# The fifth score matmul of an attention: a low-part key of 64 rows, filled up to 128 rows with zeros

## The chip, the core and the metric

The kernel runs on one core of a Trainium2 chip. The metric is the time of one execution on the device in microseconds (us), lower is better. Engines are named as in the profile: PE is TensorE's matmul stream, PEld its loads of the stationary operand, DVE is VectorE, ACT is ScalarE, POOL is GpSimd, SP is SyncE, whose queue issues most of the transfers.

## What is computed

A trunk of two layers on 512 tokens of width 2048, in float32. A layer normalises the stream, projects it, feeds three groups of heads (a gated spatial mixing A, a gated short convolution B, a latent attention C), projects the result back and adds a gated embedding. The change sits in the attention C, with 8 heads and a rotary key that all heads share:

```python
def latent_attention(q, c_kv, k_rope, z, cos, sin, kv_gain, w_ukv, qn_g, qr_g, kn_g, kr_g):
    q_nope = rms_norm(q[..., :C_NOPE], qn_g)                                # 128 features
    q_rope = apply_rope(rms_norm(q[..., C_NOPE:], qr_g), cos, sin)          # 64 features
    k_nope, v = ...                                                         # 128 features each, per head
    k_r = apply_rope(rms_norm(k_rope, kr_g), cos, sin)                      # 64 features, one for all heads
    ...
    s = jnp.einsum('bqhd,bkhd->bhqk', qn, k_nope) + jnp.einsum('bqhr,bkr->bhqk', qr, k_r)
    w = jax.nn.softmax(s.astype(jnp.float32) * scale, axis=-1)
    return jnp.einsum('bhqk,bkhd->bqhd', w, v)
```

## The kernel before

To keep float32's precision, every operand of a matmul is split into two parts of the type float32r, a high part (the rounded value, written by ACT) and a low part (what the rounding left, written by DVE). A product is then three matmuls into one PSUM bank: high by high, high by low, low by high (`mm3`, L164 to L167). Most weights are 128 x 512 tiles that come by SP's queue into five buffers (`raw`), and are split into six buffers each of `whi` and `wlo` (L144, L145).

The scores of one head for 128 queries against all 512 keys are one bank (`scores`, L606): three matmuls for the 128 features without rotation (L612 to L614) and two for the 64 rotary features (L615, L616). For these two the queries lie in `q2`, whose rows 0 to 63 are the high part and whose rows 64 to 127 are the low part of the same 64 features, and the key in `krh`, which holds the high part twice, one copy under the other. So L615, over 128 rows, makes high by high and low by high at once. L616 makes the remaining product, the high query by the low key `krl`, over rows 0 to 63 alone. In both the piece of `q2` is the stationary operand and the key is the moving one. There are 2 layers, 8 heads and 4 blocks of queries, so 64 of these banks, and L615 and L616 run 64 times each.

`krh` and `krl` are made once a layer, in `queries(0)`, long before the attention. `krl` is a tile of 128 x 512, of which only the upper 64 rows are written.

Around the scores, a generator `fillers` supplies units of 12 matmuls that don't depend on the attention (the gate z_c, and A's and B's share of the output projection); they are placed between the steps of a head by hand (`ST`, `FN`). A scheduler then sets the order of instructions on each engine, so score matmuls and fillers alternate in places. Each engine runs its own instructions in that order and waits on semaphores for the others. POOL's part in the queries is the power -1/2 of the norms (`rpow`, L232), and it issues the transfers of the attention.

Of the kernel before, what the change touches and what calls it, by code (L numbers as in the profile page):

```python
# [33 lines left out]

# columns of the input projection
OFF_U, OFF_V, OFF_ZA = 0, 512, 1024
# [8 lines left out]

# columns of the packed per-partition parameters of a layer
C_ATTN, C_PLE, C_OUT, C_KVN, C_QN, C_KN, C_CW, C_CB, C_BS = 0, 16, 32, 48, 52, 53, 54, 66, 70
NCOL = 74
# columns of the packed free-dimension gains of a layer
R_SGU, R_QR, R_KR = 0, 512, 576  # L50
NROW = 640

# 1 / 10000 ** (arange(0, 64, 2) / 64) in float32
INV_FREQ = [
# [9 lines left out]

# whole turns taken off units of 2**16 and 2**2 radians
TURNS = {2.0 ** 16: 0.37835047045272496, 2.0 ** 2: 0.6366197723675814}

NU, RAWB, HIB, SB = 62, 5, 6, 3
# units of filling work: at the start of the attention, and at the steps of a head
ST, FN = (4, 4, 4, 4, 4), (2, 1, 1, 1, 1)  # L70
# tiles of A and B that come back after each quarter of the last filler that reads the normalised input
FETCH = ((0, 1, 2, 3), (4, 5, 6, 7), (), ())
# [13 lines left out]
def trunk(ctx, tc, xT, pT, pos, freq, pars, rows, wsp, wckv, wv, w512, wq0, wq, wkv, wout, wgate, wple, outT):  # L86
# [52 lines left out]

# [1 line left out]
    def split(src, gain=None, hi=None, lo=None):  # L141
        """src (SBUF or PSUM, f32), times a per-partition gain, as two f32r parts."""
        if gain is None:
            a.copy(hi, src)  # L144
            v.tensor_tensor(out=lo, in0=src, in1=hi.bitcast(F32), op=ALU.subtract)  # L145
        else:
            a.activation(out=hi, in_=src, func=AF.Copy, scale=gain)
            v.scalar_tensor_tensor(out=lo, in0=src, scalar=gain, in1=hi.bitcast(F32),  # L148
                                   op0=ALU.mult, op1=ALU.subtract)
# [19 lines left out]
    def groupT(srcs, xs, evac, tags=("mm",)):  # L169
        """out^T: for each 128 features a bank [features, 512 tokens]; a weight unit is 4 k tiles of them."""  # L170
        nq = len(xs) // 4
        for f in range(len(srcs)):
            ps = bank(tags[f % len(tags)])
            for q in range(nq):
                wh, wl = weight(srcs[f][q], S)
                for i in range(4):
                    c = slice(i * P, (i + 1) * P)
                    k = 4 * q + i
                    mm3(ps, wh[:, c], wl[:, c], xs[k][0], xs[k][1], k == 0, k == len(xs) - 1)
            evac(f, ps)  # L180

    def groupK(srcs, load, evac):
        """the same for 4 banks at a time, a k tile at a time; a weight unit is a k tile of 512 features."""
        pb = [bank(t) for t in NB]
        for i, src in enumerate(srcs):
            xh, xl = load(i)
            wh, wl = weight(src, S)
            for f in range(4):
                c = slice(f * P, (f + 1) * P)
                mm3(pb[f], wh[:, c], wl[:, c], xh, xl, i == 0, i == len(srcs) - 1)  # L190
        for f in range(4):
            evac(f, pb[f])

    def groupN(srcs, xs, n, evac):
        """out: 4 banks [128 tokens, n features]."""
        pb = [bank(t) for t in NB]
        for i, (src, (xh, xl)) in enumerate(zip(srcs, xs)):
            wh, wl = weight(src, n)
            for t in range(NT):
                c = slice(t * P, (t + 1) * P)  # L200
                mm3(pb[t][:, :n], xh[:, c], xl[:, c], wh[:, :n], wl[:, :n], i == 0, i == len(xs) - 1)
        for t in range(NT):
            evac(t, pb[t][:, :n])

    class Stat:
        """sum over features (partitions and tiles) of squares, for each token."""

# [13 lines left out]
        def mean(self, n, eps=EPS):  # L221
            """[128 tokens, 4] of mean + eps"""
            ps = bank()
            for t in range(NT):
                pe.matmul(ps[:, t:t + 1], self.acc[:, t * P:(t + 1) * P], ones[:, 0:1], start=True, stop=True)
            m = small(NT, "mean")
            v.tensor_scalar(out=m, in0=ps[:, 0:NT], scalar1=1.0 / n, scalar2=eps, op0=ALU.mult, op1=ALU.add)
            return m
# [6 lines left out]
    def tokrow(r):  # L235
        """[128 tokens, 4] -> the same numbers along the free dimension of every partition."""
        rd = drp.tile([S], F32, name=nm("rd"))
        g.dma_start(rd.rearrange("(t p) -> p t", p=P), r)
        rt = lay.tile([P, S], F32, tag="rT", name=nm("rT"), bufs=2)
        g.dma_start(rt, rd.partition_broadcast(P))  # L240
        return rt

# [1 line left out]
    def tables():  # L244
# [41 lines left out]
        v.tensor_tensor(out=turn, in0=turn, in1=r, op=ALU.subtract)  # L286
        # radians of the coarse pieces and of the rest, then whole turns off
        v.scalar_tensor_tensor(out=turn, in0=turn, scalar=2.0 * math.pi, in1=ang, op0=ALU.mult, op1=ALU.add)
# [17 lines left out]
    def rope_gains(row, cos, sin, scale, s):  # L306
        """cos and sin times the gains of the halves that they meet."""
        out = []
# [9 lines left out]
    def rope(x, tabs, nh, outs):  # L318
        """x [P, NT, nh, 64]; outs: for each head a tile [P, NT, 2, 64], the result twice."""
        c1, s2, c2, s1 = tabs  # L320
# [15 lines left out]
    def transpose4(src):  # L336
        """four [128, 128] blocks -> one bank, side by side."""
        ps = bank()
        for t in range(NT):
            pe.transpose(ps[:, t * P:(t + 1) * P], src(t), ident)  # L340
        return ps

# [1 line left out]
    st = Stat()  # L344
# [12 lines left out]
    for L in range(DEPTH):  # L357
# [3 lines left out]

# [1 line left out]
        ck = []  # L363
# [8 lines left out]
        rT = tokrow(rN)  # L372
        # the sums lack rN: mean of the normalised input's squares is rN^2 times theirs
        m = st_k.mean(RANK, 0.0)
# [14 lines left out]

# [1 line left out]
        vh = [U("vh", F32R) for _ in range(4)]  # L391
        vl = [U("vl", F32R) for _ in range(4)]

        def rms_parts(ps, scale, segs):
            """1 / rms of the segments (offset, count, width) of scale * ps, times scale"""
            n = sum(s[1] for s in segs)
# [51 lines left out]
        def normed(tiles, r, k0):  # L448
            """normalised, with their gain, in two parts, out of the way until the output projection"""
            rt = tokrow(r)  # L450
            for i, y in enumerate(tiles):
                v.tensor_tensor(out=y, in0=y, in1=rt, op=ALU.mult)
                hi, lo = T("yh", "n", F32R), T("yl", "n", F32R)
                split(y, C(C_OUT + k0 + i), hi, lo)
                sync.dma_start(ydram[k0 + i, 0], hi.bitcast(F32))
                sync.dma_start(ydram[k0 + i, 1], lo.bitcast(F32))
# [6 lines left out]

# [1 line left out]
        if L == 0:  # L465
# [8 lines left out]
        def queries(p):  # L474
# [22 lines left out]
            if nk:  # L497
# [3 lines left out]
                a.copy(krh, ps)  # L501
                v.tensor_tensor(out=krl[0:ROPE], in0=ps[0:ROPE], in1=krh[0:ROPE].bitcast(F32), op=ALU.subtract)

# [1 line left out]
        yb = [U("yb") for _ in range(4)]  # L505
# [38 lines left out]

# [1 line left out]
        def ev_zc(f, ps):  # L546
# [6 lines left out]
        def kv(h):  # L553
            """in two parts"""
            kn = U("kn")
# [50 lines left out]
        def scores(h, half):  # L606
            (kh, kl), _, _, (qh, ql), q2 = side[h]
            pn = []
            for t in (2 * half, 2 * half + 1):
# [5 lines left out]
                pe.matmul(ps, q2[:, o], krh, start=False, stop=False)  # L615
                pe.matmul(ps, q2[0:ROPE, o], krl[0:ROPE], start=False, stop=True)  # L616
                mx = small(1, "mx")
# [12 lines left out]
        def weightsT(pn):  # L630
            """half of the queries' weights transposed, two key tiles to a bank"""
            out = []
# [34 lines left out]

        # z_c, and the share of A and B in the output projection, by units that fill the gaps of the attention
        def fillers():
# [78 lines left out]

# [1 line left out]
        st_p = Stat()  # L750
# [8 lines left out]

        # the share of C lacks its norm, which comes when it is added  # L760
        def ev_out(k, ps):
# [16 lines left out]

# [1 line left out]
        rT = tokrow(rpow(st_p.mean(D), NT))  # L780
# [32 lines left out]
def _ftiles(w):  # L813
    """[K, F] -> [F / 128, K / 512, 128, 4 * 128]: for 128 features, 4 k tiles side by side"""
    k, n = w.shape
# [58 lines left out]
```

## Time and profile before

| | |
|---|---|
| time, median of 3 runs | 2226.69 us (2224.87 to 2227.31) |
| profiled execution: span | 2231.2 us |
| PE busy | 2206.7 us (99%), 10720 matmuls |
| PEld busy | 1868.3 us (84%) |
| DVE, ACT, POOL busy | 1121.1 (50%), 906.4 (41%), 218.4 us (10%) |
| mean granted TensorE clock | 0.998 |

The profiled execution is known by its span alone, from its first to its last instruction; it is one execution, and it is 4.5 us longer than the median of the runs. Busy time of PE is not time at its peak: matmuls overlap in the pipeline, so one that takes 390 ns can start 227 ns after the one before. What the stream of matmuls costs is therefore read from the distances of their starts. The attention's scores run from about 560 to 820 us in the first layer and from about 1668 to 1932 us in the second.

### The profile page before, as it was taken

The numbers are of one execution on the slowest core, as the hardware profiler recorded it, in microseconds if no ns is written. First come the engines' busy times: TensorE is split into PE (matmuls) and PEld (weight loads), VectorE is DVE, ScalarE is ACT, GpSimd is POOL, SyncE is SP. The second block draws the span as 40 slices with busy tenths as digits, with TensorE's granted clock in tenths as the row PEclk, the third lists the DMA queues.
The fourth block names the chain that finished last, engine by engine and source line by source line (L and its number), as shares of the span: only waits on it lengthen the run. The fifth ranks groups of instructions, "written<-read, shape, count | busy, mean of one in ns | idle before, by whom it ended". The sixth has DMA issues, their size and how long they took to land.

```text
span 2231.2 us, 29725 instructions
## 1 busy us (share of the span) xinstructions
PE 2206.7 (99%) x10720; PEld 1868.3 (84%) x10720; DVE 1121.1 (50%) x2326; ACT 906.4 (41%) x1709; POOL 218.4 (10%) x331
## 2 busy tenths in 40 slices
PE   8999999999999999999999999999999999999999
PEld 6888888988888878888888888889888888888887
DVE  7444354435556655665533434444354566566433
ACT  6332333324565553443332323233246655434222
POOL 0000000002121101100000000000021221011000
PEclk9999999999999999999999999999999999999999
DMA  6333534435354444444333345334453544344432
GB/s 211 100 105 92 136 99 116 117 67 190 103 174 138 124 128 111 130 152 118 118 97 106 95 81 161 90 107 118 97 170 99 176 133 133 109 129 129 137 115 71
DMA packets 142739, 272.22 MB, mean 122 GB/s; under 512 B 17328, under 2 KB 34112, under 8 KB 142592
## 3 DMA queue, kind: packets, MB, share of 16 engines
q1 hardware_dynamic: 122256, 214.83, 33.8%
q0 software_dynamic: 18032, 51.30, 7.7%
q10 hardware_dynamic: 2304, 4.20, 0.6%
q8 instruction: 84, 1.38, 0.3%
q14 instruction: 63, 0.52, 0.1%
HBM read 234.58 MB, written 35.67 MB: 121 GB/s over the span
## 4 chain that ended last, share of the span: by engine, by line
PE 73%; DMA 3%; issue 1%; DVE 1%; ACT 0%; POOL 0%; DVEq 0%; ACTq 0%; POOLq 0%
PE mm L165 13%; PE mm L166 13%; PE mm L167 13%; PE s L167 6%; PE s L165 6%; PE s L166 6%; PE o L167 2%; PE o L166 2%; PE o L165 2%; PE tr L638 1%; PE s L616 1%; DMA ydram<-yh 1%; PE tr L340 1%; DMA rd<-rs 1%; PE s L612 1%
## 5 line engine op out<-in xcount | busy, mean ns | idle before, releaser
L145 DVE TENSOR_TENSOR wlo<-raw,whi 128x512 fp32r<-128x512 f32 (+2 forms) x754 | 501.9, 669 | 625.5 <-ACT whi L144 608.1
L144 ACT CAST whi<-raw 128x512 fp32r<-128x512 f32 (+2 forms) x754 | 449.0, 603 | 854.1 <-PE mm L166 433.0
L165 PE MATMUL mm<-hi,whi 128*128 128x512 f32 x1312 | 513.2, 391 | 3.3 <-DVE pt L387 3.3
L166 PE MATMUL mm<-lo,whi 128*128 128x512 f32 x1312 | 511.3, 390 | 0.0
L167 PE MATMUL mm<-hi,wlo 128*128 128x512 f32 x1312 | 511.1, 390 | 0.0
L165 PEld LDWEIGHTS mm<-hi,whi 128*128 128x128 f32 x1312 | 246.4, 188 | 55.1 <-issue 3.5
L167 PEld LDWEIGHTS mm<-hi,wlo 128*128 128x128 f32 x1312 | 246.3, 188 | 51.6
L166 PEld LDWEIGHTS mm<-lo,whi 128*128 128x128 f32 x1312 | 246.4, 188 | 49.5
L165 PE MATMUL s<-hi,whi 128*128 128x512 f32 x480 | 184.5, 391 | 6.8 <-ACT whi L144 5.7
L166 PE MATMUL s<-lo,whi 128*128 128x512 f32 x480 | 187.6, 391 | 1.0 <-DVE lo L148 1.0
L167 PE MATMUL s<-hi,wlo 128*128 128x512 f32 x480 | 186.4, 390 | 0.0
L166 PE MATMUL s<-wlo,hi 128*128 128x384 f32 (+2 forms) x480 | 170.6, 355 | 8.5 <-DVE wlo L145 8.5
L165 PE MATMUL s<-whi,hi 128*128 128x384 f32 (+2 forms) x480 | 169.7, 354 | 0.0
L167 PE MATMUL s<-whi,lo 128*128 128x384 f32 (+2 forms) x480 | 169.5, 353 | 0.0
L232 POOL TENSOR_TENSOR rs<-ms,mhalf 128x1 f32<-128x1 f32 (+2 forms) x104 | 87.6, 848 | 743.4 <-DVE ms L405 717.0
L165 PEld LDWEIGHTS s<-hi,whi 128*128 128x128 f32 x480 | 90.4, 189 | 25.7 <-ACT whi L144 5.7
L166 PEld LDWEIGHTS s<-lo,whi 128*128 128x128 f32 x480 | 90.6, 189 | 20.4 <-DVE lo L148 1.4
L167 PEld LDWEIGHTS s<-hi,wlo 128*128 128x128 f32 x480 | 90.1, 188 | 18.6
L166 PEld LDWEIGHTS s<-wlo,hi 128*128 128x128 f32 x480 | 90.9, 189 | 16.1 <-DVE wlo L145 10.7
L165 PE MATMUL mm<-yh,whi 128*128 128x512 f32 x256 | 103.1, 403 | 0.0
L167 PE MATMUL mm<-yh,wlo 128*128 128x512 f32 x256 | 100.4, 392 | 0.0
L166 PE MATMUL mm<-yl,whi 128*128 128x512 f32 x256 | 100.4, 392 | 0.0
(231 smaller groups left out, 3203.6 us busy)
## 6 DMA issues: line engine op xcount, KB each, us to landing
raw<-in_w_dram SPq DMA_DIRECT2D x256, 256.0 KB, 2.7
raw<-in_wout_dram SPq DMA_DIRECT2D x128, 256.0 KB, 2.8
raw<-in_wgate_dram SPq DMA_DIRECT2D x128, 256.0 KB, 2.7
raw<-in_wq_dram SPq DMA_DIRECT2D x96, 192.0 KB, 2.4
raw<-in_wckv_dram SPq DMA_DIRECT2D x32, 256.0 KB, 2.8
raw<-in_wv_dram SPq DMA_DIRECT2D x32, 256.0 KB, 2.7
raw<-in_wkv_dram SPq DMA_DIRECT2D x32, 256.0 KB, 2.8
mdram<-old SPq DMA_DIRECT2D x32, 256.0 KB, 2.0
```

What stands on the lines that cost most here:

```text
L144: a.copy(hi, src)
L145: v.tensor_tensor(out=lo, in0=src, in1=hi.bitcast(F32), op=ALU.subtract)
L165: pe.matmul(out, lh, rh, start=start, stop=False)
L166: pe.matmul(out, lh, rl, start=False, stop=False)
L167: pe.matmul(out, ll, rh, start=False, stop=stop)
L232: g.tensor_tensor(out=r, in0=m, in1=mhalf[:, 0:n], op=ALU.pow)
L340: pe.transpose(ps[:, t * P:(t + 1) * P], src(t), ident)
L612: pe.matmul(ps, qh[:, o], kh, start=True, stop=False)
L616: pe.matmul(ps, q2[0:ROPE, o], krl[0:ROPE], start=False, stop=True)
L638: pe.transpose(ps[:, j * HS + i * P:j * HS + (i + 1) * P], pn[i][:, c], ident)
```

## The change

`queries(0)` gets one more instruction: POOL writes zeros into rows 64 to 127 of `krl`. The fifth score matmul takes all 128 rows of `q2` and of `krl`: the low part of the query meets the zeros, so the sum is the same as before. Comments and docstrings go as well, which moves the lines from L504 on by one (L616 becomes L617).

```diff
                 a.copy(krh, ps)
                 v.tensor_tensor(out=krl[0:ROPE], in0=ps[0:ROPE], in1=krh[0:ROPE].bitcast(F32), op=ALU.subtract)
-
-        # ---- B: gated short convolution ----
+                g.memset(krl[ROPE:P].bitcast(F32), 0.0)
+
+
         yb = [U("yb") for _ in range(4)]
...
                 pe.matmul(ps, q2[:, o], krh, start=False, stop=False)
-                pe.matmul(ps, q2[0:ROPE, o], krl[0:ROPE], start=False, stop=True)
+                pe.matmul(ps, q2[:, o], krl, start=False, stop=True)
                 mx = small(1, "mx")
```

On PE, at the first bank of scores that is completed, the order before is this (`s` is the bank of scores, `mm` that of a filler; a row is line, operation, out<-inputs and the elements written):

```order
L166 MATMUL mm_5006<-lo_510,whi_5063 128x512
L167 MATMUL mm_5006<-hi_509,wlo_5064 128x512
L615 MATMUL s_5083<-krh_1763,q_4879 128x512
L616 MATMUL s_5083<-krl_1764,q_4879 128x512
L612 MATMUL s_5097<-hi_4799,hi_4870 128x512
L613 MATMUL s_5097<-lo_4800,hi_4870 128x512
```

In the changed kernel the same place reads as follows.

```order
L166 MATMUL mm_5007<-lo_510,whi_5064 128x512
L167 MATMUL mm_5007<-hi_509,wlo_5065 128x512
L616 MATMUL s_5084<-krh_1763,q_4880 128x512
L617 MATMUL s_5084<-krl_1764,q_4880 128x512 [waits Pool_49]
L613 MATMUL s_5098<-hi_4800,hi_4871 128x512
L614 MATMUL s_5098<-lo_4801,hi_4871 128x512
```

Nothing has moved on PE in the whole program; the first fifth matmul of a layer has a semaphore of POOL to wait for, and line numbers and tile numbers have gone up by one. On POOL, in the second layer, the place between the norms of `queries(0)` (`128x5`) and those of `queries(1)` (`128x4`) was before:

```order
L232 TENSOR_TENSOR rs_12502<-ms_12497,mhalf 128x5 [waits DVE_49]
L232 TENSOR_TENSOR rs_12517<-ms_12512,mhalf 128x5 [waits DVE_49]
L232 TENSOR_TENSOR rs_13164<-ms_13159,mhalf 128x4 [waits DVE_49,Activation_49]
L232 TENSOR_TENSOR rs_13178<-ms_13173,mhalf 128x4 [waits DVE_49,Activation_49]
L232 TENSOR_TENSOR rs_13192<-ms_13187,mhalf 128x4 [waits DVE_49]
```

And in the changed kernel:

```order
L232 TENSOR_TENSOR rs_12503<-ms_12498,mhalf 128x5 [waits DVE_49]
L232 TENSOR_TENSOR rs_12518<-ms_12513,mhalf 128x5 [waits DVE_49]
L503 MEMSET krl_11837 64x512 [waits PE_49,Pool_49]
L232 TENSOR_TENSOR rs_13166<-ms_13161,mhalf 128x4 [waits DVE_49,Activation_49,Pool_49]
L232 TENSOR_TENSOR rs_13180<-ms_13175,mhalf 128x4 [waits DVE_49,Activation_49]
```

The memset stands between the two groups, and in the second layer it waits for PE (the last reader of the buffer's contents of before). The first layer has it in the same place, without the wait for PE. No other row of DVE, ACT, POOL or SP has another place than before.

## Rows read from the trace of the kernel before

**Rows 1.** Head of the page, and its part 1: busy time of the engines.

```profile
span 2231.2 us, 29725 instructions
## 1 busy us (share of the span) xinstructions
PE 2206.7 (99%) x10720; PEld 1868.3 (84%) x10720; DVE 1121.1 (50%) x2326; ACT 906.4 (41%) x1709; POOL 218.4 (10%) x331
```

**Rows 2.** Busy time by stretches; (x) instructions, PEclk granted clock, DMA share, GB/s.

```profile
560.00:945.00 385.00, 385.00 (x1983) 317.65 (x1982) 228.25 (x488) 202.54 (x395) 59.71 (x100) 1.00 0.44 130
1667.00:1945.00 278.00, 278.00 (x1501) 228.80 (x1501) 161.49 (x376) 159.74 (x323) 48.34 (x80) 1.00 0.43 133
```

**Rows 3.** Tile krl: its instructions, duration ns min/median/max, idle time before.

```profile
L616 PEld LDWEIGHTS s<-krl,q x64: 182/183/183, 572.6 to 1932.4; 64*128 64x128 f32 x64
L616 PE MATMUL s<-krl,q x64: 491/498/502, 572.6 to 1932.4; 64*128 64x512 f32 x64
L502 DVE TENSOR_TENSOR krl<-tr,krh x2: 681/682/683, 294.1 to 1399.7; 64x512 fp32r<-64x512 f32 x2
...
  issue: 20.8, 64
```

**Rows 4.** Line L615: duration ns min/median/max.

```profile
L615 PEld LDWEIGHTS s<-krh,q x64: 186/188/190, 572.1 to 1931.8; 128*128 128x128 f32 x64
L615 PE MATMUL s<-krh,q x64: 388/397/502, 572.3 to 1932.0; 128*128 128x512 f32 x64
```

**Rows 5.** Timeline of PE around the first fifth matmul: start us, us, line.

```profile
565.29 0.39 PE L167 MATMUL mm<-hi,wlo 128*128 128x512 f32 x1
...
572.09 0.39 PE L167 MATMUL mm<-hi,wlo 128*128 128x512 f32 x1
572.31 0.39 PE L615 MATMUL s<-krh,q 128*128 128x512 f32 x1
572.63 0.50 PE L616 MATMUL s<-krl,q 64*128 64x512 f32 x1
573.06 0.50 PE L612 MATMUL s<-hi,hi 128*128 128x512 f32 x1
573.39 0.39 PE L613 MATMUL s<-lo,hi 128*128 128x512 f32 x1
```

**Rows 6.** Timeline of PEld, same place; in brackets idle before it.

```profile
572.63 0.18 PEld L616 LDWEIGHTS s<-krl,q 64*128 64x128 f32 x1 [0.35 <-issue]
573.06 0.19 PEld L612 LDWEIGHTS s<-hi,hi 128*128 128x128 f32 x1 [0.25 <-issue]
```

**Rows 7.** Timeline of PE, another place, three fifth matmuls close together.

```profile
680.61 0.47 PE L615 MATMUL s<-krh,q 128*128 128x512 f32 x1
...
683.50 0.40 PE L166 MATMUL mm<-yl,whi 128*128 128x512 f32 x1
```

**Rows 8.** Waits of PEld, 560 to 945 us: total us, times, longest.

```profile
PEld s L616 <- issue: 10.4, 32, 0.4
PEld mm L165 <- issue: 3.4, 14, 0.2
...
```

**Rows 9.** Waits of all engines, 560 to 945 us.

```profile
ACT whi L144 <- PE mm L166: 54.0, 36, 3.0
```

**Rows 10.** Timeline of all engines, 652 to 662 us; in brackets idle before it.

```profile
652.92 0.72 ACT L147 ACTIVATE hi<-yc,par 128x512 fp32r<-128x512 f32 x1 [1.60 <-DVE yc L654]
...
661.00 0.36 ACT L573 ACTIVATE kn<-mm,rs 128x128 f32<-128x128 f32 x1
...
662.01 0.27 PE L340 MATMUL tr<-ident,kn 128*128 128x128 f32 x1
```

**Rows 11.** Groups of POOL's instructions by form: busy us, mean ns.

```profile
L125 POOL MEMSET ones<- 128x128 f32 x1 | 0.2, 202 | 0.0
L127 POOL MEMSET mhalf<- 128x32 f32 x1 | 0.1, 121 | 0.0
```

**Rows 12.** Timeline of POOL, second layer, between queries(0) and queries(1).

```profile
1461.55 1.98 POOL L232 TENSOR_TENSOR rs<-ms,mhalf 128x4 f32<-128x4 f32 x2 [72.96 <-DVE ms L405]
```

## The prediction

> **What bounds the kernel now.** I read the page's head first: a span of 2231.2 us with PE busy for 2206.7 us of it, so PE sits without a matmul for 24.5 us in all, while no other engine is busy for more than half [rows 1]. Then the table by stretches, for the two in which the scores run: PE is busy for 385.00 of 385.00 us and for 278.00 of 278.00 us, at a granted clock of 1.00, which is the upper level, 2.4 GHz [rows 2]. There nothing is late for PE; what counts is how fast its matmuls follow one another. Busy time doesn't show that, since matmuls overlap, so the third view is the list by line, and the fourth the timeline, from which I take distances of starts.
>
> The list by line sets L616 and L615 side by side. Both write 128 x 512 outputs with 512 moving columns and the same `q2` block as stationary operand. L616 reads half the rows, yet takes 491 to 502 ns where L615 has a median of 397 ns; its weight load is the same as the other's, 183 against 188 ns, but stands behind 20.8 us of idle time of the loads in 64 cases, 0.325 us each, with nothing waited for that the profile shows ("issue") [rows 3, 4].
>
> **What a fifth matmul costs now.** An undisturbed matmul of 512 columns first: from the L167 at 565.29 to that at 572.09 us there are 30 matmuls, so 6.80 / 30 = 0.227 us from start to start [rows 5]. Then around the first L616: L615 starts at 572.31, L616 at 572.63 (0.32 later), L612 at 573.06 (0.43), L613 at 573.39 (0.33). These three steps last 1.08 us; three undisturbed ones would last 3 x 0.227 = 0.68. So 0.40 us is lost around one L616 [rows 5].
>
> The loads say how. In a run of 128-row matmuls a load lies beside the matmul before it. The load for L616 comes at 572.63, together with its own matmul and 0.32 us after L615's start, and the load for L612 at 573.06, again together with its matmul; both have idle time ahead (0.35 and 0.25 us) [rows 6]. So when the stream goes from 128 rows to 64 and when it goes back, PE no longer loads ahead, as if the running matmul had to come to its end first; the load is exposed, twice per L616. That it is the number of rows I take from what else differs: L615 and L616 have the same stationary block, engine and bank, and no semaphore is named ahead of L616. That a bank is finished by it isn't it either: the L167 at 572.09 ends a filler's bank, and L615 follows 0.22 us later [rows 5].
>
> The Trainium skill, "TensorEngine Tiling (Array Packing)", section "Key Properties", says that a change of the tiling mode drains TensorE, and "Available Configurations" has 64 x 128 among the modes; the trace agrees, 0.40 us around one pair of changes. The same notes say in "TensorE: Matmul & The Clock Gate", section "LDWEIGHTS (loading the stationary operand)", that a load's time goes by its columns and not by the contraction, which speaks against the change; the trace agrees for the load itself (183 and 188 ns), so by this rule alone the time would stay 2226.7 us.
>
> It is so in all 64 places. In the first layer's stretch the loads of L616 have 10.4 us of "issue" in 32 cases, and behind them stands, beside the score matmuls that follow, L165 of a filler with 3.4 us in 14 [rows 8]. Where three L616 stand close together, with an L615 between each two, the time from the first L615 (680.61) to the L166 behind the third (683.50) is 2.89 us for seven steps, against 7 x 0.227 = 1.59. Of the 1.30 us between them about 0.10 belongs to the transposes ahead, after which the first L615 takes 0.47 us in place of 0.39; the other 1.2 us are three times 0.40 [rows 7].
>
> **The change part by part.** (1) The fifth matmul takes 128 rows, as its neighbours do. It then has the shape, the operands' types and the place of L615, and I cost it as an undisturbed matmul: 0.227 us, and no pause on either side. That is 64 x 0.40 = 25.6 us off PE's stream. The order on PE is the same, so nothing else is gained or lost there. Its bounds: read to 0.01 us the three steps may be 1.07 or 1.09, so 64 x 0.39 = 25.0 and 64 x 0.41 = 26.2 us. (2) The zeros: one memset a layer on POOL. POOL's memsets show 202 ns for 128 columns and 121 ns for 32 [rows 11], 0.84 ns a column, so about 0.53 us for 512 (estimate from these two rows); from below it is 0.2. It stands where POOL is idle for 72.96 us, until the powers that start at 1461.55 us [rows 12]. Nothing waits for it until the first score. Price 0; without this cover it would be twice 0.53 us. (3) The added wait of PE on POOL, at the first fifth matmul of a layer, is for a memset that must be over before the powers at 1461.55 us, some 200 us ahead of the second layer's stretch at 1667 [rows 2, 12]. Price 0. (4) What is late next. The weights follow PE by themselves: ACT's casts wait for PE to release buffers, 54.0 us in 36 places of the first stretch [rows 9], so a faster PE is supplied sooner. The tightest place that I found in the attention is the transpose of `kn` at 662.01 us. ACT works without a gap from 652.92 us on (two table loads among it) and finishes that `kn` at 661.00 + 0.36 = 661.36, 0.65 us before PE gets there [rows 10]. Two L616 lie in this stretch, so PE would come 0.80 us sooner and wait 0.15 us. The second layer repeats it. I book 2 x 0.15 = 0.3 us against the gain, and up to 2 us at the range's upper end for places that I didn't see.
>
> The sum: 25.6 - 0.3 = 25.3 us. The profiled execution becomes 2231.2 - 25.3 = 2205.9 us in span; it is 4.5 us longer than the median of the runs, 2226.69 us, and what lies outside its span isn't recorded, so I take the same 25.3 us off the median: 2201.4 us.
>
> **The rivals.** *Only one side of the pause goes.* If what follows L616 belongs to something else than its rows, only the way in is saved, 0.32 - 0.227 = 0.09 us, 64 x 0.09 = 6 us: 2220.7; if only the way out, 0.20 + 0.11 = 0.31 us, 20 us: 2206.9. Against it stands that the pauses follow L616 whatever comes next, a score or a filler [rows 8]. *Nothing goes:* the pause belongs to the fifth matmul's place, or to going over to another key tile, and 128 rows wait in the same way: 2226.7. For it speaks only that the loads take equally long [rows 3, 4], against it that L615, in the same place but for one, has no pause ahead when it follows a 128-row matmul (0.22 us at 572.31) [rows 5]. The Trainium skill's rule on the columns of a load, taken alone, ends here too. *PE is free, but its inputs are not:* ACT and DVE, with 202.54 and 228.25 us of 385 [rows 2], hold it up in more places like that of `kn`. All 64 pauses would have to be eaten for no gain; half of them give 2214. *Slower:* in the second layer the memset waits for the PE matmul that last read its buffer, on POOL's in-order queue, and behind it stand the powers of `queries(1)`, without which PE's banks aren't released. It costs from the moment at which that wait ends after 1461.55 us, and makes the kernel slower by over 0.2% if it ends after 1461.55 + 25.3 + 4.5 = 1491 us. Against it: the subtraction that writes the other half of the same buffer, and needs the same release, runs at 1399.7 us already [rows 3].
>
> **How the numbers follow.** A measurement of this kernel can tell about 0.2%, 4.5 us, from no change. Full gain 0.87; one side only 0.05 (both ends of it faster); inputs late 0.03 (faster); nothing 0.03 (same); slower 0.02. Faster is then 0.95. The time is that of the full gain, 2201.4 us. The range: the largest gain, 26.2 us, from the fastest of the runs, 2224.87, gives 2198.7; the smallest, 25.0, less 2 us of new waits, from the slowest, 2227.31, gives 2204.3; I go to 2198.5 and 2205.0, which leaves out the rivals and little else.
>
> **What would show it.** Right: the fifth matmul's line (now L617) at 390 to 400 ns and its load beside the matmul before it; 0.22 to 0.23 us from the fourth matmul's start to the fifth's and on; the "issue" idle time of its loads gone; the attention's two stretches shorter by about 12.8 us each, and nothing else moved; a wait of a few tenths of a us at the transposes of `kn`. Wrong: a fifth matmul that still starts over 0.3 us after the fourth; new waits of PE of more than 2 us between 560 and 830 or 1650 and 1920 us; POOL's powers after `queries(0)` later than now.

## The result and the profile after

The changed kernel takes 2198.91 us (median of 4 runs, 2197.75 to 2199.84) against 2226.12 us before (4 runs, 2224.87 to 2227.31): a ratio of 0.9879, with a 95% interval of 0.9865 to 0.9893. Timed again on another occasion it takes 2199.28 us against 2224.81 us (21 runs of before), a ratio of 0.9885 (0.9871 to 0.9898). That is 25 to 27 us less; 25.3 were forecast, and 2201.4 us (2198.5 to 2205.0).

The page's head and its part 1 answer to [rows 1]:

```profile
span 2198.1 us, 29729 instructions
## 1 busy us (share of the span) xinstructions
PE 2180.6 (99%) x10720; PEld 1872.6 (85%) x10720; DVE 1119.8 (51%) x2326; ACT 905.0 (41%) x1709; POOL 221.0 (10%) x333
```

As many matmuls as before, and PE is as full as before, but 26.1 us shorter. The tile `krl` answers to [rows 3] (duration ns min/median/max, first and last start in us):

```profile
L617 PEld LDWEIGHTS s<-krl,q x64: 187/188/192, 567.6 to 1899.3; 128*128 128x128 f32 x64
L617 PE MATMUL s<-krl,q x64: 387/392/398, 567.9 to 1899.5; 128*128 128x512 f32 x64
L503 POOL MEMSET krl<- x2: 522/522/523, 279.3 to 1370.3; 64x512 f32 x2
```

The fifth matmul has gone from 498 to 392 ns, and the line on idle time ("issue: 20.8, 64" before) isn't there any more. The timeline of PE at the same place as [rows 5]:

```profile
567.41 0.39 PE L167 MATMUL mm<-hi,wlo 128*128 128x512 f32 x1
567.64 0.39 PE L616 MATMUL s<-krh,q 128*128 128x512 f32 x1
567.86 0.39 PE L617 MATMUL s<-krl,q 128*128 128x512 f32 x1
568.09 0.39 PE L613 MATMUL s<-hi,hi 128*128 128x512 f32 x1
568.32 0.39 PE L614 MATMUL s<-lo,hi 128*128 128x512 f32 x1
```

The three steps from the fourth matmul (567.64) to the one two behind the fifth (568.32) last 0.68 us, where they lasted 1.08. The loads, against [rows 6], lie beside the matmul ahead of theirs again, with no idle time in brackets:

```profile
567.41 0.19 PEld L616 LDWEIGHTS s<-krh,q 128*128 128x128 f32 x1
567.64 0.19 PEld L617 LDWEIGHTS s<-krl,q 128*128 128x128 f32 x1
567.87 0.19 PEld L613 LDWEIGHTS s<-hi,hi 128*128 128x128 f32 x1
```

POOL, against [rows 12], with the first layer in the first two lines and the second in the others:

```profile
279.27 0.52 POOL L503 MEMSET krl<- 64x512 f32 x1
352.21 1.98 POOL L232 TENSOR_TENSOR rs<-ms,mhalf 128x4 f32<-128x4 f32 x2 [72.42 <-ACT whi L144]
...
1370.28 0.52 POOL L503 MEMSET krl<- 64x512 f32 x1
1443.21 1.98 POOL L232 TENSOR_TENSOR rs<-ms,mhalf 128x4 f32<-128x4 f32 x2 [72.41 <-ACT whi L144]
```

The memset takes 0.52 us and runs right behind the powers of `queries(0)`, so its wait for PE in the second layer was over by then; POOL still idles for 72.4 us behind it.

How much of the whole is made in the attention, is read from the fifth matmuls of the first layer alone, from the first start to the last. Before and after, the rows of the tile `krl` in that layer are these:

```profile
L616 PE MATMUL s<-krl,q x32: 491/498/502, 572.6 to 824.5; 64*128 64x512 f32 x32
```

```profile
L617 PE MATMUL s<-krl,q x32: 387/392/398, 567.9 to 807.2; 128*128 128x512 f32 x32
```

These are 251.9 us before and 239.3 after. The timelines have the last of them to 0.01 us, first before and then after:

```profile
824.48 0.50 PE L616 MATMUL s<-krl,q 64*128 64x512 f32 x1
...
807.18 0.39 PE L617 MATMUL s<-krl,q 128*128 128x512 f32 x1
```

From 572.63 to 824.48 are 251.85 us, from 567.86 to 807.18 are 239.32: 12.53 us less, with 31 steps from one fifth matmul to the next, so 0.404 us a step (12.53 / 31). The second layer, from 1680.5 to 1932.4 and from 1660.2 to 1899.5 us, has the same lengths. For 64 fifth matmuls this makes 64 x 0.404 = 25.9 us.

### The profile page after: what moved, and what is told of

Read it like the earlier page. It is cut to its first block, busy times and chain, and to the rows that moved or that the text cites. A ratio compares the mean times of both kernels' runs of the same rounds, so it can differ in the third digit from the quotient of the medians.

```text
span 2198.1 us, 29729 instructions
## 1 busy us (share of the span) xinstructions
PE 2180.6 (99%) x10720; PEld 1872.6 (85%) x10720; DVE 1119.8 (51%) x2326; ACT 905.0 (41%) x1709; POOL 221.0 (10%) x333
## 4 chain that ended last, share of the span: by engine, by line
PE 74%; DMA 2%; issue 1%; DVE 1%; POOL 0%; ACT 0%; DVEq 0%; ACTq 0%; POOLq 0%
PE mm L165 13%; PE mm L166 13%; PE mm L167 13%; PE s L167 6%; PE s L165 6%; PE s L166 6%; PE o L166 2%; PE o L167 2%; PE o L165 2%; PE tr L639 1%; PE tr L340 1%; PE tr L166 1%; PE tr L167 1%; PE tr L165 1%; PE s L615 1%
## 5 line engine op out<-in xcount | busy, mean ns | idle before, releaser
L165 PE MATMUL mm<-hi,whi 128*128 128x512 f32 x1312 | 512.7, 391 | 1.1 <-DVE pt L387 1.0
L166 PE MATMUL mm<-lo,whi 128*128 128x512 f32 x1312 | 511.3, 390 | 0.0
L165 PEld LDWEIGHTS mm<-hi,whi 128*128 128x128 f32 x1312 | 246.4, 188 | 52.0 <-DVE pt L387 1.2
L166 PEld LDWEIGHTS mm<-lo,whi 128*128 128x128 f32 x1312 | 246.4, 188 | 49.8
L165 PE MATMUL s<-hi,whi 128*128 128x512 f32 x480 | 184.5, 391 | 5.9 <-ACT whi L144 5.7
L166 PE MATMUL s<-lo,whi 128*128 128x512 f32 x480 | 187.7, 391 | 0.9 <-DVE lo L148 0.9
L166 PE MATMUL s<-wlo,hi 128*128 128x384 f32 (+2 forms) x480 | 170.2, 355 | 4.7 <-DVE wlo L145 4.7
L165 PE MATMUL s<-whi,hi 128*128 128x384 f32 (+2 forms) x480 | 169.5, 353 | 0.0
L165 PEld LDWEIGHTS s<-hi,whi 128*128 128x128 f32 x480 | 90.4, 189 | 25.2 <-ACT whi L144 5.7
L166 PEld LDWEIGHTS s<-lo,whi 128*128 128x128 f32 x480 | 90.5, 189 | 20.0 <-DVE lo L148 1.4
L165 PE MATMUL mm<-yh,whi 128*128 128x512 f32 x256 | 101.5, 396 | 0.0
L166 PEld LDWEIGHTS s<-wlo,hi 128*128 128x128 f32 x480 | 90.8, 189 | 10.9 <-DVE wlo L145 5.4
L166 PE MATMUL mm<-yl,whi 128*128 128x512 f32 x256 | 100.1, 391 | 0.0
```

The source lines that it names most:

```text
L165: pe.matmul(out, lh, rh, start=start, stop=False)
L166: pe.matmul(out, lh, rl, start=False, stop=False)
```

## The experiments

The theory: a passage of PE's stream from 128-row to 64-row matmuls and back costs 0.40 us (a "passage" is always the way in and the way back together), and the change saves 64 of them and nothing else. The rivals: the gain is from elsewhere (the memset, the wait, chance); any difference in rows makes the pause; each 64-row matmul pauses by itself.

**The kernel before against itself.** No edit.

> The kernel before, unchanged, timed against itself: both theories expect the same time, 2226 us within 2 us. Its profile shows how much the parts that the change does not touch (the projections ahead of the attention) differ from one execution to the next: the change's profile was 33.1 us shorter in span than that of before, of which 25.9 us lie at the 64 fifth matmuls. If the other 7 us are chance, this profile's stretch before the first score differs from the first one's by some us too.

2225.33 us against 2224.81, ratio 1.0001 (0.9992 to 1.0010): the comparison tells a difference of 0.1%, some 2 us, from none. The profile of this run is the one to set beside the first:

```profile
span 2220.9 us, 29725 instructions
...
L616 PE MATMUL s<-krl,q x32: 491/498/502, 567.5 to 819.4; 64*128 64x512 f32 x32
```

The scores of a layer take 251.9 us again, but the first of them starts 5.1 us sooner than in the first profile (567.5, 572.6). So 10.3 us of that profile's span of 2231.2 us were chance, in stretches that the change doesn't touch; PE's wait for `wlo` at L166, the largest of its waits, was 8.5 us there and is 4.0 us here. The difference of the two first spans, 33.1 us, overstates the change.

**The changed kernel, timed again.** No edit.

> The changed kernel, timed again. Row theory (a passage from 128 to 64 rows and back costs 0.40 us on PE, and nothing else changed): 64 x 0.404 = 25.9 us less than before, so 2200.2 us. Rival (something beside the fifth matmul was gained as well): 27 us or more less, 2199 us or less, clearly outside 25.9 +- 0.5.

2199.28 us, 25.5 us less than 2224.81, with an interval of the ratio (0.9871 to 0.9898) that is 22.7 to 28.7 us. The 25.9 us of the theory lie in its middle, so a gain beside them isn't needed; but the rival's 27 us lie in it too, and this timing doesn't part the two. The profiles do: the span less the two stretches from a layer's first fifth matmul to its last is 1727.4, 1717.1 and 1720.0 us in the three profiles with 64 rows (the kernel before, that kernel again, zeros alone) and 1719.5, 1719.4 and 1721.2 us in the three with more (the changed kernel, that kernel again, 96 rows). Outside the scores nothing was gained that stands out from chance.

**Zeros written, but 64 rows.**

```diff
                 v.tensor_tensor(out=krl[0:ROPE], in0=ps[0:ROPE], in1=krh[0:ROPE].bitcast(F32), op=ALU.subtract)
+                g.memset(krl[ROPE:P].bitcast(F32), 0.0)
```

> The zeros are written, but the fifth matmul stays at 64 rows. Row theory: the time of before, 2226 us within 2 us, and idle time of about 0.33 us ahead of each load of the fifth matmul as before. Rival (the gain comes from what the memset moves, or from the added wait): about 2200 us.

2224.95 us, ratio 0.9999 (0.9991 to 1.0008). The tile `krl` in its profile:

```profile
L617 PE MATMUL s<-krl,q x64: 491/498/503, 568.9 to 1924.9; 64*128 64x512 f32 x64
L503 POOL MEMSET krl<- x2: 522/522/522, 280.3 to 1383.9; 64x512 f32 x2
...
  issue: 20.8, 64
```

Matmul and idle time are those of before (but for 1 ns in the longest), though the memset is there: it costs and gains nothing that this comparison, good to 0.1%, can tell. The added wait of PE for POOL isn't in this run, since the fifth matmul reads the upper 64 rows alone; it is in the changed kernel, where the load of the first fifth matmul still starts with the fourth matmul, at 567.64 us.

**96 rows.**

```diff
-                pe.matmul(ps, q2[0:ROPE, o], krl[0:ROPE], start=False, stop=True)
+                pe.matmul(ps, q2[0:96, o], krl[0:96], start=False, stop=True)
```

with zeros in rows 64 to 95 only.

> The fifth matmul takes 96 rows, with zeros in rows 64 to 95. Row theory in its narrow form (64 rows are a mode of the array of their own, 96 go as 128 do): the time of the changed kernel, about 2199 to 2200 us, no idle time ahead of the loads. Rival (every change of the number of rows between neighbours makes the pause): 2226 us, with the pause.

2199.30 us, ratio 0.9883 (0.9868 to 0.9898): the time of the changed kernel. The timeline of PE around the first fifth matmul:

```profile
569.92 0.39 PE L616 MATMUL s<-krh,q 128*128 128x512 f32 x1
570.15 0.40 PE L617 MATMUL s<-krl,q 96*128 96x512 f32 x1
570.38 0.40 PE L613 MATMUL s<-hi,hi 128*128 128x512 f32 x1
570.62 0.40 PE L614 MATMUL s<-lo,hi 128*128 128x512 f32 x1
```

A matmul of 96 rows between two of 128 makes no pause: 0.70 us for the three steps, against 0.68. So it isn't a difference in rows as such; 64 rows are something of their own, 96 aren't. The Trainium skill's list of modes in "TensorEngine Tiling (Array Packing)", "Available Configurations", has 64 rows and 32, and none between 64 and 128; the trace agrees, with 0.70 us at 96 rows. No run here tries 32.

**64 rows, in pairs.** The fifth matmuls of two blocks are issued together, behind the other four of both.

```diff
+            pss = []
             for t in (2 * half, 2 * half + 1):
...
                 pe.matmul(ps, q2[:, o], krh, start=False, stop=False)
-                pe.matmul(ps, q2[0:ROPE, o], krl[0:ROPE], start=False, stop=True)
+            for t in (2 * half, 2 * half + 1):
+                o = slice(t * P, (t + 1) * P)
+                pe.matmul(pss[t % 2], q2[0:ROPE, o], krl[0:ROPE], start=False, stop=True)
+            for ps in pss:
                 mx = small(1, "mx")
```

> Fifth matmul with 64 rows as before, but issued for two blocks of queries together, so that in 20 places two of them follow each other directly: 44 passages into 64 rows and back in place of 64. Row theory (the passage costs, not the matmul): 20 x 0.40 = 8 us less than before, 2218 us. Rival (each 64-row matmul pauses on its own account): no change, 2226 us.

2219.47 us against 2224.83, 5.4 us less, ratio 0.9976 (0.9967 to 0.9986), that is 3.1 to 7.3 us. The sign is the theory's; its 8 us lie just outside the interval. A pair, in its profile's timeline of PE (x2: two matmuls in one row):

```profile
569.10 0.39 PE L617 MATMUL s<-krh,q 128*128 128x512 f32 x1
569.42 0.73 PE L620 MATMUL s<-krl,q 64*128 64x512 f32 x2
570.08 0.50 PE L165 MATMUL mm<-hi,whi 128*128 128x512 f32 x1
570.41 0.40 PE L166 MATMUL mm<-lo,whi 128*128 128x512 f32 x1
```

From 569.10 to 570.41 are four steps, 1.31 us; undisturbed they are 4 x 0.227 = 0.91. So two 64-row matmuls lose 0.40 us together, as one did. From a layer's first fourth matmul to its last (568.19 to 816.39 us) are 248.2 us, against 251.8 before (572.31 to 824.16): 3.65 us less, where ten passages make 4.0. Two layers give 7.3 us, the upper end of the interval. The span less these two stretches is 1720.0 us, amid those of the kernel before, so no loss outside the scores is shown; why the whole gave 5.4 us stays open (chance is enough for it).

**64 rows, in halves of 256 columns.**

```diff
-                pe.matmul(ps, q2[0:ROPE, o], krl[0:ROPE], start=False, stop=True)
+                for j in range(2):
+                    w = slice(j * HS, (j + 1) * HS)
+                    pe.matmul(ps[:, w], q2[0:ROPE, o], krl[0:ROPE, w], start=False, stop=j == 1)
```

> Fifth matmul with 64 rows, in two halves of 256 columns each, so 128 matmuls of 64 rows in 73 passages (9 pairs are parted by the scheduler). Row theory: 9 x 0.40 = 3.6 us more for passages and about 1 us for 128 short matmuls in place of 64 long ones, 2230.5 us. Rival (each 64-row matmul pauses on its own account): 64 more pauses of 0.40 us, about 2252 us.

2228.66 us against 2224.83, 3.8 us more, ratio 1.0017 (1.0008 to 1.0026), 1.8 to 5.8 us. The theory has 4.6 us more, the rival some 26. By the profile there are 73 passages, as expected ("issue: 22.3, 73" for the loads of `krl`). The timeline of PE:

```profile
568.22 0.39 PE L615 MATMUL s<-krh,q 128*128 128x512 f32 x1
568.53 0.50 PE L618 MATMUL s<-krl,q 64*128 64x256 f32 x2
568.96 0.50 PE L612 MATMUL s<-hi,hi 128*128 128x512 f32 x1
569.30 0.40 PE L613 MATMUL s<-lo,hi 128*128 128x512 f32 x1
```

Two 64-row matmuls in a row, and the stretch from L615 to L613 is the 1.08 us of one before. A passage is paid once, whether it holds one 64-row matmul or two.

**No fifth matmul.** From the changed kernel; the product of the high query and the low key is left out.

```diff
-                pe.matmul(ps, q2[:, o], krh, start=False, stop=False)
-                pe.matmul(ps, q2[:, o], krl, start=False, stop=True)
+                pe.matmul(ps, q2[:, o], krh, start=False, stop=True)
```

> The changed kernel without its fifth matmul; the product of the high query and the low key is left out. Row theory: in the changed kernel the fifth matmul costs no more than an undisturbed one, 64 x 0.227 = 14.5 us, so 2184.5 us. Rival (128 rows keep a part of the pause): more is saved, with 0.1 us of pause left 64 x 0.33 = 21 us, 2178 us.

2191.81 us, ratio 0.9852 (0.9839 to 0.9866): 7.5 us less than the changed kernel's 2199.28, neither the 14.5 of the theory nor the rival's 21. The scheduler also set part of the work in another order here. Its waits of PE show where time was given back (total us, times, longest):

```profile
PE mm L165 <- ACT kn L574: 2.6, 2, 1.3
PE mm L165 <- DVE h L767: 2.3, 2, 2.0
```

The first of these isn't among the changed kernel's, and the second neither. In a layer the scores, now taken from the fourth matmuls, last 569.2 to 802.9 us, 233.7, against 567.6 to 806.9, 239.3, in the changed kernel: 5.6 us less. With the 1.3 us of wait for `kn` put back these are 6.9 us over 31 steps, 0.223 us a step. So the fifth matmul of the changed kernel costs what an undisturbed one costs, but only half of what leaving it out frees reaches the end: of the missing 7.0 us, 4.9 stand in these two waits on ACT and DVE, and 2.1 stay open (the new order of work, or chance).

## Why the prediction was right

**The price of a passage.** 0.40 us, read from one place and multiplied by 64, was right: 12.53 us over 31 steps in each layer. Read to three digits it is 0.404, which makes 25.9 us in place of 25.6. The reason given, the number of rows and not the place, the block or the end of a bank, holds: with the zeros alone nothing changes, with 96 rows all of the gain comes, and pairs and halves show that the passage costs and not the matmul. That the running matmul is let to end first is how the starts look; the traces show no drain as such.

**The memset and the wait.** Both were priced at 0. For the memset the ratio of 0.9999 with the zeros alone bears it out; for the wait, which that run doesn't have, the changed kernel's trace does, with no wait of PE in either layer's scores. The estimate of 0.53 us for the memset, from two other sizes, met 0.52. The rival of a memset that holds up POOL in the second layer fell with the row at 1370.28 us.

**The wait at `kn`** was the step that failed. I booked 0.15 us a layer; the changed kernel has no wait of PE between 540 and 840 us at all. The changed kernel's timeline there is this:

```profile
652.38 0.36 ACT L574 ACTIVATE kn<-mm,rs 128x128 f32<-128x128 f32 x1
...
652.49 0.27 PE L340 MATMUL tr<-ident,kn 128*128 128x128 f32 x1
```

The transpose starts while ACT is still at this write, so it doesn't wait for it: ACT writes `kn` in four pieces for four groups of tokens, and this transpose reads one that was written earlier. I had set the last write of the tile against its first read. The fourth transpose of this head, which by the order of the pieces reads that last write, stands much later:

```profile
659.34 0.28 PE L340 MATMUL tr<-ident,kn 128*128 128x128 f32 x1
```

That is 6.6 us behind the end of the write (652.38 + 0.36). In the trace of before it starts at 668.86 us, 7.5 us behind 661.36, where the prediction saw 0.65. So the predicted wait of a few tenths of a us at the transposes couldn't come. PE does begin to wait for this write in the run without the fifth matmul, but with another instruction and for another reason:

```profile
653.70 0.37 ACT L574 ACTIVATE kn<-mm,rs 128x128 f32<-128x128 f32 x1
...
654.13 0.50 PE L165 MATMUL mm<-yh,whi 128*128 128x512 f32 x1 [1.28 <-ACT kn L574]
```

This L165 is a filler's and doesn't read `kn`; by its operands what it needs is a bank `mm`, such as this write of ACT reads. In that run's order ACT comes to the write later, too, behind the copies of `e`. That the prediction named the same write is luck.

**Nothing given back.** In the attention PE waits for nothing after the change, as before it, so the gain stayed whole. A next gain would not: of 14.5 us by leaving out the fifth matmul 7.5 came through, and 4.9 went into waits.

**Span and median.** I took the gain off both. Off the long profile's span it made 2205.9 us, where the span after is 2198.1: the profile of before was an unusually long execution, 2231.2 us where the other recorded ones of that kernel have spans of 2220.8 to 2226.1. (A run's time is some 1.8 us above its span in every recorded run, 2199.84 for 2198.1, so it was longer than the median by some 6 us and not 4.5.) Off the median the forecast came out 2.5 us too high: 0.6 us are the wait booked at `kn` and the rounding, and 1.9 us the median of 2226.69, which three runs gave and 21 later ones put at 2224.81. The 2198.91 us lie 0.4 us above the range's lower end, with single runs below it; that the median fell inside owes something to luck.

## What to carry to other kernels

Read a matmul's cost from the distance of the starts around it, three or four steps wide, not from its own duration: here 0.1 us of extra duration stood for 0.40 us of stream. Here a matmul over 64 rows amid matmuls over 128 was dearer, by 0.40 us, than the same one filled up with zeros. Where rows to fill are at hand, try that; where not, try putting 64-row matmuls together, since two of them paid for one passage (more than two weren't tried). And after a gain on the bound engine, look which inputs now come last before counting on the next.

## What was not expected of the hardware

A matmul over 96 rows costs next to nothing more than one over 128: 392/395/403 ns against 387/392/398, and a layer's fifth matmuls from 570.1 to 810.1 us, 240.0 long against 239.3. Inside a pair of 64-row matmuls the second starts 0.34 us after the first (0.73 - 0.39 in the pair's row), not 0.227, yet the pair loses no more than a single one. The starts say how: the pair's four steps are 0.32, 0.34, 0.32 and 0.33 us, so about 0.1 us is lost ahead of the first matmul of either kind and about 0.1 us behind it, at the way in and again at the way back. Around a single 64-row matmul (0.32, 0.43, 0.33 in [rows 5]) the second and third of these losses fall into one step, 0.227 + 0.2. What PE does in each wasn't tried.
